# Sums of squares moved between TensorE, POOL and ACT in a four-layer trunk, with a new order of the first loads and of the first projections

## The chip, the cores and the metric

The kernel runs on one core of one Trainium2 chip. The metric is the device time of one execution in microseconds (us), as the median of several runs. The engines are called PE (TensorE matmul), PEld (its weight loads), DVE (VectorE), ACT (ScalarE), POOL (GpSimd) and SP (SyncE, which here only starts transfers).

## The reference

x is 512 positions by 1024 channels in float32. Four layers with the mixers A (Conformer convolution), B (forgetting attention), C (short gated convolution) and A again each add their output to x:

```
hn = rms_norm(x, norm[i]);  x = x + mixer_i(hn)
A: val, gate, z = split(hn @ w_in)            # 3 x 2048 columns
   u = conv31(val * sigmoid(gate)) + b
   u = silu(layer_norm(u, g, b));  out = (u * silu(z)) @ w_out
B: q, k, v, z, f = split(hn @ w_in)           # 16 heads of 128
   q, k = rms_norm(q), rms_norm(k)            # over the 128 of a head
   c = cumsum(log_sigmoid(f + b))
   o = causal softmax(q.k/sqrt(128) + c[t] - c[s]) @ v;  out = (o * silu(z)) @ w_out
C: u, b, c, z = split(hn @ w_in);  out = (b * conv3(c * u) * silu(z)) @ w_out
```

So every layer needs the mean of x squared per position, the A layers also the mean and the mean square of 2048 channels (for layer_norm), and every head of B the mean of q squared and of k squared.

## The kernel before

**Tiles.** Channels lie on the 128 partitions, positions along the free axis. x is 8 tiles of 128x512; the 2048 inner channels are 16 tiles of 128x512. A sum over channels is a sum over partitions and tiles, and is made on PE by a matmul with a matrix of equal constants (`ones_d`, `ones_e`, `ones_h`, and `ones_hr` in fp32r).

**Products in two parts.** Each fp32 operand of a large product is split into a high part in fp32r and the rest, also fp32r. A product is hi·hi + hi·lo + lo·hi: 3 groups of 8 matmuls of 128x512, 24 in all, for each chunk of weights. A chunk of 128x1024 weights is loaded into `w_raw` by SP (a ring of AHEAD = 3), ACT casts it to `w_hi`, and POOL (or DVE) subtracts to give `w_lo` (L413); these two have rings of 4.

**Norms ahead of their sum.** The h of a layer (`hh`, `hl`: x times the norm's gain, split in two) doesn't hold the factor rstd = 1/rms. In B and C the results are multiplied by rstd afterwards. In A only the first four projections (`raw_tiles` = 2: val_0, gate_0, val_1, gate_1) are so treated; from the fifth on, val_2, the operand is `hn` = x·gain·rstd, made by `normalise` once rstd is there. `Stream.add` makes hh, hl and the square of each tile of x, and `norm` sums the squares with `ms` matmuls in fp32 and takes the reciprocal root (ACT Ln and Exp, then three steps on DVE, the last writes `rstdp`).

**Layer A.** The convolution of 31 taps runs as DVE operations (`cv`) and on POOL (`pacc`), a few tiles on PE (`conv_pe`, whose matrices `pw` are loaded by SP). `count_in` adds up each tile's sum and square: POOL sums into s1 and s2, or the tile goes to PE of itself. At the end PE makes `meanp` and `e2p` with fp32 matmuls, and from these come the factor `lnrp`, and per tile `d` → times lnrp → SiLU → times sz → `g_hi`, `g_lo`, which the out projection `o` reads.

**Layer B.** For every head `queries` projects q, takes its square's sum `qs` (L379, by 4 products that have one column of `ones_h` as moving operand) and from it the factor `qr`; `normalise` does the same for k with `ks`. Logits `lg` for four blocks of queries (3 down to 0) give p_3 to p_0 on DVE and ACT; they are scaled by 1/sum on DVE (`rsum`, L350), transposed on PE into `pt`, split, and multiplied with v into `op`.

**Order.** Every operation is handed to a planner (`Plan`). It has a cost for each operation and engine, a priority (place in the program plus `boost`), and the engines that may take it; it simulates the kernel once when it is built, and writes out a fixed order for each engine. An engine works its row in that order, and each instruction waits for what it reads. So any edited cost, boost or engine can move every row behind it.

Of the kernel before, what the change touches and what calls it, by code (L numbers as in the profile page):

```python
# [14 lines left out]
A = mybir.AluOpType  # L15
# [235 lines left out]
def trunk(ctx: ExitStack, tc: tile.TileContext, x, w, vec, pw, out):  # L251
# [41 lines left out]
    def pe_time(n):  # L293
        return max(0.108, 0.0105 + n * 0.4225e-3)
# [100 lines left out]
    def load_chunk():  # L395
        n = state["load"]
        b = plan.buf(lambda: stage.tile([P, 1024], F32, tag="w_raw", name=f"w_raw{n}",
                                        bufs=AHEAD), "w_raw", AHEAD)
        plan.op({"dma": 1.5}, lambda e: nc.sync.dma_start(b(), w[n]), w=[b], boost=-4000 if n >= AHEAD else 0)
        raw_ring[n] = b  # L400
        state["load"] += 1
# [70 lines left out]
    def project(dst, h, fine=False, boost=0):  # L472

        hi, lo = chunk()
        hh, hl = h
        for g, (a, b) in enumerate(((hi, hh), (hi, hl), (lo, hh))):
            for ks in ([k] for k in range(ND)) if fine else [range(ND)]:
                ks = list(ks)
                mms(lambda a=a, b=b, g=g, ks=ks: [
                        (dst(), a()[:, k * P : (k + 1) * P], b[k](),  # L480
                         g == 0 and k == 0, g == 2 and k == ND - 1) for k in ks],
                    [dst], pe_time(T) * len(ks), [a, *(b[k] for k in ks)], boost)

    class Stream:
# [8 lines left out]
        def add(self, d):  # L493
# [7 lines left out]
            act(sq, xs[d], AF.Square, boost=40 if self.layer == 0 else 0)  # L501
            if self.layer == 0 or d in (0, ND - 1):
                self.squares.append(sq)
            else:
                tt(("pool", "dve"), self.squares[0], self.squares[0], sq, A.add)
# [61 lines left out]
    def conformer(layer, st):  # L567
        lo_engines["now"] = ("pool",)
        on_pe = PE_TILES[layer]
        FIRST, EARLY = 2, 7  # L570
        raw_tiles, SPREAD, SHIFTED, DIRECT = 2, 12, 4, 2

        def cw(i, s):
            return v(f"conv_w{layer}", i * KC + KC - 1 - s)

        s1, s2, m0 = slot("s1"), slot("s2"), slot("m0")
        us, d2, sz, last = {}, {}, {}, []
# [75 lines left out]
        def count_in(i):  # L653
# [56 lines left out]
        mp, ep = psum("o", "meanp"), psum("sum", "e2p")  # L710
        for n, (a, b) in enumerate(zip([s1] + [d2[i] for i in range(NE - DIRECT, NE)],
                                       [s2] + last)):
            for dst, src in ((mp, a), (ep, b)):
                mms(lambda n=n, dst=dst, src=src: [
                    (dst(), ones_e(), src(), n == 0, n == DIRECT)], [dst], 0.86, [ones_e, src],
                    boost=-2000)
# [26 lines left out]
    def attention(layer, st):  # L743
# [61 lines left out]
        def queries(h):  # L805
# [6 lines left out]
            act(qh, acc, AF.Copy, scale=g, boost=-200)  # L812
            stt(ql, acc, g, qh, A.mult, A.subtract, boost=-200, b_f32r=True)
            ms = psum("sum", f"qs{h}")
            mms(lambda: [(ms()[:, col(j)], sq()[:, blk(j)], ones_h()[:, :1], True, True)
                         for j in range(NB)], [ms], 0.6, [sq, ones_h])
            m, r, t = fq[h % 2]

            def tiny(op, *bufs, w):
                plan.op({"dve": 0.17}, lambda _: op(), bufs, [w])  # L820
            tiny(lambda: nc.vector.tensor_tensor(m(), ms()[:, :NB], rt2(), A.mult), ms, rt2, w=m)
            plan.op({"act": 0.25}, lambda _: nc.scalar.activation(r(), m(), AF.Ln, bias=eps_t()),
# [219 lines left out]
```

## Time and profile before

| | before |
|---|---|
| median of 3 runs | 1793.65 us (1792.62 to 1793.85) |
| the profiled execution's own time | 1794.22 us |
| its span in the trace | 1792.3 us |
| granted TensorE clock, mean | 0.999 |
| POOL, w_lo, 128x1024 | 274 of 2414 ns |
| ACT, w_hi, 128x1024 | 289 of 1050 ns |
| DVE, cv | 608 of 736 ns |

A line of the profile gives the line of the code, the engine, the operation, written tile <- read tiles, their shape, how often (x), then times. In the lines by time the first number is the start in us from the span's start, the second how long the row lasted (for a row with x3, from the first start to the last end), and in brackets stands idle time ahead of it and what ended that.

The layers lie about so in the span: A from 0 to 402 us, B to 962 (its 16 heads from 410 to 880), C to 1394, A to the end.

### The profile page before, as it was taken

The page shows a single profiled execution, that of the slowest core. Times are in us where ns is not written, and L with a number is a line of the kernel's source. Part 1 is how long each engine was busy: PE and PEld are TensorE (multiplying, and loading weights), DVE is VectorE, ACT ScalarE, POOL GpSimd, SP SyncE. Part 2 cuts the span into 40 slices and gives each one's busy share as a digit, 9 for nine tenths or more (in the row PEclk, how much of TensorE's full clock was granted, in tenths as well). Part 3 has the DMA queues.
Part 4 walks back from the last instruction along what each step waited for, and adds up shares of the span by engine and source line. Part 5 has one row for each costly group of instructions (what it writes and reads, how often), then busy time and mean ns, then how long its engine had stood idle before and what let it go on. Part 6 is the DMA issues. An engine that isn't in the chain of part 4 may idle for free.

```text
span 1792.3 us, 21883 instructions
## 1 busy us (share of the span) xinstructions
PE 1767.3 (99%) x8196; PEld 1462.4 (82%) x8196; DVE 1167.2 (65%) x1690; ACT 866.7 (48%) x1255; POOL 1096.9 (61%) x654
## 2 busy tenths in 40 slices
PE   8999999999999999999999999999999999999999
PEld 6788887888888888888788888888888878878787
DVE  6999997736777777867523333333313699999770
ACT  6656655536555555656433222222223564755550
POOL 5999998865333333544454555455445599989882
PEclk9999999999999999999999999999999999999999
DMA  6243432233222222222222222222223224334222
GB/s 219 83 154 99 141 135 83 94 106 118 83 78 91 85 77 85 75 77 71 71 95 94 94 94 100 101 94 95 96 100 123 88 94 147 106 129 136 94 94 71
DMA packets 63065, 182.40 MB, mean 102 GB/s; under 512 B 7136, under 2 KB 13280, under 8 KB 62960
## 3 DMA queue, kind: packets, MB, share of 16 engines
q1 hardware_dynamic: 62960, 181.02, 29.9%
q8 instruction: 64, 1.05, 0.2%
q14 instruction: 41, 0.34, 0.1%
HBM read 175.71 MB, written 5.28 MB: 101 GB/s over the span
## 4 chain that ended last, share of the span: by engine, by line
PE 81%; DVE 16%; POOL 1%; issue 1%; DMA 1%; ACT 0%; SPq 0%; DVEq 0%; POOLq 0%; ACTq 0%
PE o L379 19%; PE z L379 17%; DVE cv L341 13%; PE k L379 5%; PE v L379 5%; PE u L379 5%; PE c L379 5%; PE b L379 5%; PE q L379 5%; PE gate L379 3%; PE val L379 3%; PE cv L379 2%; PE op L379 2%; PE lg L379 2%; PE pt L874 1%
## 5 line engine op out<-in xcount | busy, mean ns | idle before, releaser
L413 POOL TENSOR_TENSOR w_lo<-w_raw,w_hi 128x1024 fp32r<-128x1024 f32 x274 | 661.1, 2414 | 586.2 <-PE z L379 110.0
L315 ACT CAST w_hi<-w_raw 128x1024 fp32r<-128x1024 f32 x289 | 303.2, 1050 | 550.9 <-issue 137.1
L341 DVE SCALAR_TENSOR_TENSOR cv<-u,vt,cv 128x495 f32<-128x495 f32 (+24 forms) x608 | 447.2, 736 | 19.7
L330 POOL TENSOR_TENSOR pacc<-prod,pacc 128x510 f32<-128x510 f32 (+5 forms) x148 | 174.7, 1181 | 11.1 <-ACT prod L317 4.4
L330 DVE TENSOR_TENSOR x<-o,x 128x512 f32<-128x512 f32 x32 | 21.2, 687 | 200.9 <-PE o L379 200.9
L317 ACT ACTIVATE prod<-u,vt 128x510 f32<-128x510 f32 (+8 forms) x166 | 106.9, 709 | 46.3 <-DVE u L330 46.3
L379 PE MATMUL o<-g_hi,w_hi 128*128 128x512 f32 x512 | 127.9, 391 | 0.7 <-DVE z L330 0.7
L379 PE MATMUL o<-g_lo,w_hi 128*128 128x512 f32 x512 | 127.0, 389 | 0.0
L379 PE MATMUL o<-g_hi,w_lo 128*128 128x512 f32 x512 | 126.7, 389 | 0.0
L379 PEld LDWEIGHTS o<-g_hi,w_hi 128*128 128x128 f32 x512 | 95.8, 188 | 21.7 <-DVE z L330 1.5
L379 PEld LDWEIGHTS o<-g_hi,w_lo 128*128 128x128 f32 x512 | 96.0, 188 | 19.9
L379 PEld LDWEIGHTS o<-g_lo,w_hi 128*128 128x128 f32 x512 | 95.9, 188 | 19.8
L246 ACT ACT_TABLE_LOAD x70 | 89.8, 1283 | 1.9 <-PEq L1030 0.7
L330 DVE TENSOR_TENSOR z<-z,rstd 128x512 f32<-128x512 f32 x32 | 22.1, 691 | 90.2 <-PE z L379 90.1
L379 PE MATMUL z<-hn_hi,w_hi 128*128 128x512 f32 x256 | 65.8, 400 | 2.2 <-ACT sz L317 2.2
L379 PE MATMUL z<-hl,w_hi 128*128 128x512 f32 x256 | 64.6, 394 | 0.0
L379 PE MATMUL z<-hn_hi,w_lo 128*128 128x512 f32 x256 | 64.3, 393 | 0.0
L379 PE MATMUL z<-hh,w_hi 128*128 128x512 f32 x256 | 64.0, 392 | 0.0
L379 PE MATMUL z<-hn_lo,w_hi 128*128 128x512 f32 x256 | 63.7, 391 | 0.0
L379 PE MATMUL z<-hh,w_lo 128*128 128x512 f32 x256 | 63.3, 389 | 0.0
L379 PEld LDWEIGHTS z<-hn_hi,w_hi 128*128 128x128 f32 x256 | 48.1, 191 | 13.9 <-ACT sz L317 3.8
L341 DVE SCALAR_TENSOR_TENSOR hl<-x,vt,hh 128x512 fp32r<-128x512 f32 x32 | 47.6, 1508 | 16.6 <-ACT hh L317 16.6
(245 smaller groups left out, 3708.1 us busy)
## 6 DMA issues: line engine op xcount, KB each, us to landing
w_raw<-w SPq DMA_DIRECT2D x289, 512.0 KB, 3.3
pw<-pw SPq DMA_DIRECT2D x54, 256.0 KB, 4.5
nc<-cd SPq DMA_DIRECT2D x16, 256.0 KB, 3.6
x<-x SPq DMA_DIRECT2D x8, 256.0 KB, 5.2
out<-x SPq DMA_DIRECT2D x8, 256.0 KB, 3.7
ud<-ua SPq DMA_DIRECT2D x6, 256.0 KB, 2.0
phases<-ud SPq DMA_DIRECT2D x24, 64.0 KB, 2.5
od<-oa SPq DMA_DIRECT2D x6, 256.0 KB, 3.9
```

The lines of the kernel that those rows point to most:

```text
L246: switch(table)
L315: nc.scalar.copy(of(dst, d), of(src, s))
L317: nc.scalar.activation(of(dst, d), of(src, s), func, **kw)
L330: eng[e].tensor_tensor(of(dst, d), of(a, s), of(b, sb), op)
L341: nc.vector.scalar_tensor_tensor(of(dst, d), of(a, s), c, bb.bitcast(F32) if b_f32r else bb, op0, op1)
L379: nc.tensor.matmul(o, a, b, start=start, stop=stop)
L413: eng[e].tensor_tensor(lo(), raw(), hi().bitcast(F32), A.subtract)
L874: nc.tensor.transpose(tp()[:, blk(i - j)], p[i]()[:, blk(j)], ident())
```

## The change

1. `queries`: q's square is split into `sq_hi` (ACT) and `sq_lo` (POOL only), and the sum is made by 8 matmuls with two columns of the fp32r constants instead of 4 fp32 products with one column. Its planned cost goes from 0.6 to 0.5 us.
2. `Stream.add`: fewer squares go to PE of themselves. In layer 0 tiles 1 to 3 are added to tile 0's by POOL or DVE (8 `ms` matmuls become 5); in B and C all are added (2 become 1); in the last A layer it stays at 2.
3. `conformer`: of the convolution's 16 tiles only the last one that isn't made on PE (`late`, tile 14) goes to the sums directly, instead of tiles 14 and 15. `meanp` and `e2p` take 2 matmuls each instead of 3.
4. `project` with `fine` (the first projection of each layer): part 7 of h is taken last in all three groups.
5. `load_chunk`: the high priority of a load of weights begins with chunk 6 instead of 3.

```
-        plan.op({"dma": 1.5}, lambda e: nc.sync.dma_start(b(), w[n]), w=[b], boost=-4000 if n >= AHEAD else 0)
+        plan.op({"dma": 1.5}, lambda e: nc.sync.dma_start(b(), w[n]), w=[b], boost=-4000 if n >= 2 * AHEAD else 0)
...
-        for g, (a, b) in enumerate(((hi, hh), (hi, hl), (lo, hh))):
-            for ks in ([k] for k in range(ND)) if fine else [range(ND)]:
-                ks = list(ks)
...
+        groups = list(enumerate(((hi, hh), (hi, hl), (lo, hh))))
+        order = [(g, range(ND)) for g in groups]
+        if fine:
+            order = [(g, [k]) for g in groups for k in range(ND - 1)]
+            order += [(g, [ND - 1]) for g in groups]
+        for (g, (a, b)), ks in order:
...
-            if self.layer == 0 or d in (0, ND - 1):
+            if d == 0 or self.layer == 0 and d >= ND // 2 or LAYERS[self.layer] == "A" and d == ND - 1:
                 self.squares.append(sq)
             else:
                 tt(("pool", "dve"), self.squares[0], self.squares[0], sq, A.add)
...
+        late = max(i for i in range(NE) if i not in on_pe)
...
-            if i < NE - DIRECT:
+            if i != late:
                 tt(("pool",), s1, s1, d2[i], A.add)
                 tt(("pool",), s2, s2, sq, A.add)
...
-        for n, (a, b) in enumerate(zip([s1] + [d2[i] for i in range(NE - DIRECT, NE)],
-                                       [s2] + last)):
+        for n, (a, b) in enumerate(zip([s1, d2[late]], [s2] + last)):
             for dst, src in ((mp, a), (ep, b)):
                 mms(lambda n=n, dst=dst, src=src: [
-                    (dst(), ones_e(), src(), n == 0, n == DIRECT)], [dst], 0.86, [ones_e, src],
+                    (dst(), ones_e(), src(), n == 0, n == 1)], [dst], 0.86, [ones_e, src],
...
+            sp = split(sq, "sq", ("pool",))
             ms = psum("sum", f"qs{h}")
-            mms(lambda: [(ms()[:, col(j)], sq()[:, blk(j)], ones_h()[:, :1], True, True)
-                         for j in range(NB)], [ms], 0.6, [sq, ones_h])
+            mms(lambda: [(ms()[:, 2 * j : 2 * j + 2], b()[:, blk(j)], ones_hr()[:, :2],
+                          b is sp[0], b is sp[1]) for j in range(NB) for b in sp],
+                [ms], 0.5, [*sp, ones_hr])
```

The planner then orders nearly everything anew. Three places matter below.

First, PE at the start of the program. `val_0` is the first projection, `sq` are the squares of the tiles of x, `gate_0` is the second projection. Before, from the eighth row on:

```order
L379 MATMUL ms_139<-sq_146,ones_d_73 128x512
L379 MATMUL val_0_48_126<-hh_5_36_158,w_hi_106 128x512
L379 MATMUL val_0_48_126<-hh_6_39_165,w_hi_106 128x512
L379 MATMUL val_0_48_126<-hh_7_42_171,w_hi_106 128x512
L379 MATMUL val_0_48_126<-hl_0_22_118,w_hi_106 128x512
L379 MATMUL ms_139<-sq_176,ones_d_73 128x512
L379 MATMUL ms_139<-sq_181,ones_d_73 128x512
L379 MATMUL val_0_48_126<-hl_1_25_124,w_hi_106 128x512
L379 MATMUL ms_139<-sq_192,ones_d_73 128x512
L379 MATMUL val_0_48_126<-hl_2_28_135,w_hi_106 128x512
```

Now, the end of val_0 and what follows:

```order
L379 MATMUL val_0_48_126<-hh_7_42_165,w_hi_106 128x512
L379 MATMUL val_0_48_126<-hl_7_43_172,w_hi_106 128x512
L379 MATMUL val_0_48_126<-hh_7_42_165,w_lo_112 128x512
L379 MATMUL ms_209<-sq_122,ones_d_73 128x512
L379 MATMUL ms_209<-sq_201,ones_d_73 128x512
L379 MATMUL ms_209<-sq_207,ones_d_73 128x512
L379 MATMUL ms_209<-sq_211,ones_d_73 128x512
L379 MATMUL ms_209<-sq_216,ones_d_73 128x512
L379 MATMUL gate_0_78_233<-hh_0_21_110,w_hi_178 128x512
```

The eight `ms` matmuls stood between those of val_0; the five now stand in one piece behind it and ahead of gate_0, and the first of them reads sq_122, the sum of four tiles' squares.

Second, POOL at the same place, right behind its constants. Before, its first five rows with work are all low parts of weights (chunks 0 to 4):

```order
L413 TENSOR_TENSOR w_lo_112<-w_raw_96,w_hi_106 128x1024
L413 TENSOR_TENSOR w_lo_161<-w_raw_137,w_hi_153 128x1024
L413 TENSOR_TENSOR w_lo_194<-w_raw_169,w_hi_186 128x1024
L413 TENSOR_TENSOR w_lo_207<-w_raw_183,w_hi_197 128x1024
L413 TENSOR_TENSOR w_lo_254<-w_raw_214,w_hi_234 128x1024
```

Now:

```order
L413 TENSOR_TENSOR w_lo_112<-w_raw_96,w_hi_106 128x1024
L330 TENSOR_TENSOR sq_122<-sq_122,sq_160 128x512
L330 TENSOR_TENSOR sq_122<-sq_122,sq_169 128x512
L413 TENSOR_TENSOR w_lo_191<-w_raw_158,w_hi_178 128x1024
L413 TENSOR_TENSOR w_lo_213<-w_raw_174,w_hi_193 128x1024
```

Two of the three additions stand ahead of the second chunk's low part; the third, `sq_122<-sq_122,sq_186`, stands on DVE behind its eight `hl`.

Third, DVE in a head of B (the third one). `p_3` to `p_0` are the four blocks of the softmax, scaled here by 1/sum; `k_606<-k_605` (now `k_614<-k_613`) is the next head's k projection times rstd. Before:

```order
L350 TENSOR_SCALAR p_2_580_4380<-p_2_580_4380,rsum_435_3867 128x384
L866 RECIPROCAL rsum_434_3877<-rsum_434_3877 128x1
L350 TENSOR_SCALAR p_1_582_4403<-p_1_582_4403,rsum_434_3877 128x256
L866 RECIPROCAL rsum_433_3881<-rsum_433_3881 128x1
L350 TENSOR_SCALAR p_0_584_4422<-p_0_584_4422,rsum_433_3881 128x128
L330 TENSOR_TENSOR k_606_4462<-k_605_4392,rstd_453_3538 128x512
```

Now:

```order
L350 TENSOR_SCALAR p_2_586_4404<-p_2_586_4404,rsum_435_3876 128x384
L330 TENSOR_TENSOR k_614_4484<-k_613_4416,rstd_453_3538 128x512
L871 RECIPROCAL rsum_434_3896<-rsum_434_3896 128x1
L350 TENSOR_SCALAR p_1_588_4427<-p_1_588_4427,rsum_434_3896 128x256
L871 RECIPROCAL rsum_433_3898<-rsum_433_3898 128x1
L350 TENSOR_SCALAR p_0_590_4451<-p_0_590_4451,rsum_433_3898 128x128
```

The k row, which needs the end of a projection on PE, has moved ahead of p_1 and p_0. It is so in every second head; in the others the old order stays. In every head the chunk of v's weights, whose low part DVE made before, now has it made by POOL (11 low parts go from DVE to POOL), and POOL makes the low part of q's square too.

More of the change, by code (lines that the diff above doesn't have):

```diff
@@ L475, in project @@
         hh, hl = h
-        for g, (a, b) in enumerate(((hi, hh), (hi, hl), (lo, hh))):
-            for ks in ([k] for k in range(ND)) if fine else [range(ND)]:
-                ks = list(ks)
[L479 to L482, printed above, removed]
+        groups = list(enumerate(((hi, hh), (hi, hl), (lo, hh))))
[4 more added lines that the diff above has]
+        for (g, (a, b)), ks in order:
+            mms(lambda a=a, b=b, g=g, ks=ks: [
+                    (dst(), a()[:, k * P : (k + 1) * P], b[k](),
+                     g == 0 and k == 0, g == 2 and k == ND - 1) for k in ks],
+                [dst], pe_time(T) * len(ks), [a, *(b[k] for k in ks)], boost)
     class Stream:
@@ L570, in conformer @@
         FIRST, EARLY = 2, 7
-        raw_tiles, SPREAD, SHIFTED, DIRECT = 2, 12, 4, 2
+        raw_tiles, SPREAD, SHIFTED = 2, 12, 4
         def cw(i, s):
             return v(f"conv_w{layer}", i * KC + KC - 1 - s)
+        late = max(i for i in range(NE) if i not in on_pe)
         s1, s2, m0 = slot("s1"), slot("s2"), slot("m0")
@@ L820, in tiny @@
                 plan.op({"dve": 0.17}, lambda _: op(), bufs, [w])
-            tiny(lambda: nc.vector.tensor_tensor(m(), ms()[:, :NB], rt2(), A.mult), ms, rt2, w=m)
+            tiny(lambda: nc.vector.tensor_tensor(m(), ms()[:, : 2 * NB : 2], rt2(), A.mult), ms, rt2, w=m)
             plan.op({"act": 0.25}, lambda _: nc.scalar.activation(r(), m(), AF.Ln, bias=eps_t()),
```

## The prediction

> **What bounds the kernel now.** I read the page's busy times first, then its chain that ended last, both shares of the span of 1792.3 us:
>
> ```profile
> PE 1767.3 (99%) x8196; PEld 1462.4 (82%) x8196; DVE 1167.2 (65%) x1690; ACT 866.7 (48%) x1255; POOL 1096.9 (61%) x654
> ...
> PE 81%; DVE 16%; POOL 1%; issue 1%; DMA 1%; ACT 0%; SPq 0%; DVEq 0%; POOLq 0%; ACTq 0%
> ```
>
> PE is busy in 99% of the span, and the chain lies on it. Only DVE has a share beside it. Where, the view by stretches of the span tells (columns: PE, PEld, DVE, ACT, POOL busy, clock, DMA share, GB/s; the stretches are a part of the first A layer, the heads of B, B's out projection with the first matmuls of C, and C):
>
> ```profile
> 130.00:263.00 133.00, 130.16 (x623) 108.22 (x622) 126.62 (x176) 84.84 (x108) 123.80 (x90) 1.00 0.38 127
> 406.00:880.00 474.00, 470.14 (x2342) 395.01 (x2341) 352.58 (x654) 278.23 (x487) 191.73 (x96) 1.00 0.25 83
> 880.00:964.00 84.00, 84.00 (x377) 69.52 (x377) 20.36 (x22) 27.10 (x34) 44.06 (x20) 1.00 0.28 94
> 964.00:1312.00 348.00, 348.00 (x1534) 287.54 (x1532) 130.12 (x148) 87.24 (x97) 170.41 (x83) 1.00 0.29 97
> ```
>
> In C PE alone is full (348.00 of 348). In A DVE (126.62 of 133) and POOL (123.80) are nearly full too, so their queues decide small waits. In B DVE has room on average, but the softmax is a chain of latencies between PE's products. So PE work that goes away is won, as long as no DVE or POOL result that PE needs comes later by as much.
>
> **The prices.** The critical chain at the start prices the fp32 sum of squares and a projection:
>
> ```profile
> 17.67 2.57 PE ms L379 x6
> 20.25 2.54 PE val L379 x11
> 22.79 5.44 PE gate L379 x24
> ```
>
> A matmul over 512 columns in fp32 is two records (x6 is three): 2.57 / 3 = 0.857 us each. An fp32r matmul is 5.44 / 24 = 0.227 us. The change removes 3 `ms` in layer 0, one each in B and C, and two of `meanp`/`e2p` in each A layer: 9 x 0.857 = **7.7 us** of PE work.
>
> q's squares, before, behind the last logits of a head (PE, then PEld):
>
> ```profile
> 442.65 0.22 PE L379 MATMUL lg<-k_hi,q_hi 128*128 128x128 f32 x1
> 442.71 0.28 PE L379 MATMUL lg<-k_lo,q_hi 128*128 128x128 f32 x1
> 442.82 0.27 PE L379 MATMUL lg<-k_hi,q_lo 128*128 128x128 f32 x1
> 442.94 1.00 PE L379 MATMUL qs<-ones_h,sq 128*128 128x1 f32 x8
> 443.80 1.64 PE L379 MATMUL k<-hl,w_hi 128*128 128x512 f32 x6
> ...
> 442.88 0.97 PEld L379 LDWEIGHTS qs<-ones_h,sq 128*128 128x128 f32 x8
> ```
>
> From 442.94 to 443.80 the 8 passes take 0.86 us, 0.108 each; each must load 128 columns of squares as weights. The new form has 8 fp32r passes with 8 such loads. The nearest rows for those are the logits, fp32r with 128 columns: 0.11 us from start to start (442.71, 442.82, 442.94), also set by the weight load. So 8 x 0.11 = 0.88 against 0.86: **0.0 us**. The best end is 0.06 (442.65 to 442.71 follows a wide matmul, whose time had covered the load): 16 x 8 x 0.05 = 6.4 us won; no reason allows a worse end.
>
> The Trainium skill, page "TensorE: Matmul & The Clock Gate", section on weight-path performance modes, says that fast weight load comes on by itself when 128 weights are loaded and the type isn't FP32. If fp32r counted as another type, the new loads would be quicker than the old ones, and the sum would be by the 0.06 end. The logits' 0.11 in fp32r speaks against it.
>
> **Sums in B and C (-1.7 us).** These lose one `ms` each. The first projection f of B and the POOL work beside it:
>
> ```profile
> 402.79 2.39 POOL L413 TENSOR_TENSOR w_lo<-w_raw,w_hi 128x1024 fp32r<-128x1024 f32 x1 [3.05 <-PE o L379]
> ...
> 406.99 1.98 PE L379 MATMUL f<-hh,w_lo 128*128 128x512 f32 x8
> 408.82 1.02 PE L379 MATMUL ms<-sq,ones_d 128*128 128x512 f32 x2
> ```
>
> The one `ms` now waits for the last addition on POOL. POOL is free at 405.2, an addition takes 1.27 (below), so it ends near 406.5; `ms` is wanted behind f near 408. f's cover of some 1.5 us hides it. -2 x 0.857 = -1.7; if a POOL low part (2.4) came ahead of the addition, 0.9 would be paid in each, +1.8 at worst.
>
> **Statistics in A (-3.4, +0.7).** Two `meanp`/`e2p` go in each A layer: -4 x 0.857 = -3.4. But the four left stand later: 64 matmuls of z lie between them and the out projection, before 80. That is 16 x 0.227 = 3.6 us less for the chain to g. Its slack before:
>
> ```profile
> 298.03 2.54 POOL L330 TENSOR_TENSOR d<-d,mean 128x512 f32<-128x512 f32 x2 [4.45 <-DVE mean L720]
> ...
> 324.70 6.88 DVE L366 TENSOR_TENSOR g_lo<-d,g_hi 128x512 fp32r<-128x512 f32 x4
> ...
> 328.14 1.98 PE L379 MATMUL o<-g_lo,w_hi 128*128 128x512 f32 x8
> ```
>
> The four g_lo (tiles 4 to 7) take 1.72 each, so tile 5's is done at 328.1; PE wants it as the fifth of its eight, at 328.14 + 4 x 0.227 = 329.05. Slack 0.9. The first row prices an addition on POOL, 1.27. In the new order POOL has one low part (2.4) less between the statistics and g_5, so 3.6 - 2.4 - 0.9 = 0.35 us is lost in each A layer: +0.7, between 0 and 2 x 2.7 if that low part doesn't matter.
>
> **The start (+2.5).** Before:
>
> ```profile
> 12.02 3.67 DVE L341 SCALAR_TENSOR_TENSOR hl<-x,vt,hh 128x512 fp32r<-128x512 f32 x3 [0.48 <-ACT hh L317]
> 22.45 0.69 DVE L341 SCALAR_TENSOR_TENSOR nt<-nt,rstd 128x512 f32<-128x512 f32 x1
> 23.18 2.77 DVE L341 SCALAR_TENSOR_TENSOR rstdp<-nt,rstd 128x512 f32<-128x512 f32 x1
> ...
> 22.93 2.47 POOL L413 TENSOR_TENSOR w_lo<-w_raw,w_hi 128x1024 fp32r<-128x1024 f32 x1 [2.69 <-PE val L379]
> ...
> 11.26 1.95 ACT L317 ACTIVATE hh<-x,vt 128x512 fp32r<-128x512 f32 x3
> 16.57 1.67 ACT L317 ACTIVATE sq<-x 128x512 f32<-128x512 f32 x3
> 20.34 0.69 ACT L317 ACTIVATE rstd<-ms,eps_t 128x512 f32<-128x512 f32 x1 [2.10 <-PE ms L379]
> ...
> 22.63 1.75 PE L379 MATMUL gate<-hh,w_hi 128*128 128x512 f32 x7
> ...
> 38.95 1.98 PE L379 MATMUL val<-hn_hi,w_hi 128*128 128x512 f32 x8
> ```
>
> Two things are to be seen. PE gets all of h only at 15.7 (12.02 + 3.67), so the eight `ms` lay partly in val_0's waits. And `rstdp`, which takes two operands from SBUF, lasted 2.77 instead of the 0.69 of `nt`, its like: it ended at 25.95, where POOL's low part had ended at 25.40. A DVE operation of that kind waits for the POOL instruction that runs.
>
> Now val_0 ends at 15.7 + 2 x 0.227, near 16.2. ACT's new row has the first w_hi (to 5.8), eight hh (0.65 each), two sq (0.56), a third, a w_hi (1.0) and the fourth sq: the second sq comes near 11.8, the third near 13.0, the fourth near 14.5. The sum of squares needs two POOL additions (1.27 each, from 11.8 to near 14.4) and one on DVE. This has two SBUF operands and the fourth square, when POOL has just begun the next low part (2.4): it ends at 17.4 to 18.4. Five `ms` (4.3 us) make gate_0 start at 21.7 to 22.7, before 22.63, and the root start near 22.6, before 20.34. So nothing is won for gate_0, and 2.3 us are lost for hn. In the new DVE row the last hn stands behind `raw` of gate_1, whose end is near 38.9, and behind the u made from it: `raw` 0.69, the sigmoid on ACT 0.65, u 0.69 and hn_7 0.69 end near 41.6, its high part near 42.3, and near 42.5 with some tenths between the engines. val_2 wants it at 38.9 + 7 x 0.227 = 40.5: a wait of 2, before none. With the spread of gate_0's start I take +2.5. Ends: -2 (DVE's addition gets in ahead of the low part) and +6 (another low part lies before it and before rstdp).
>
> Part 7 of h taken last and the early x loads are in this sum. In the other layers I put part 7 at nothing: in 880 to 964, which ends in C's first projection, PE is busy in all 84.00 us.
>
> **The heads of B (+6).** Before, DVE and POOL around the end of a k projection, and the last head:
>
> ```profile
> 502.93 0.35 DVE L350 TENSOR_SCALAR p<-p,rsum 128x256 f32<-128x256 f32 x1
> ...
> 503.39 0.29 DVE L350 TENSOR_SCALAR p<-p,rsum 128x128 f32<-128x128 f32 x1
> 505.34 0.69 DVE L330 TENSOR_TENSOR k<-k,rstd 128x512 f32<-128x512 f32 x1 [1.66 <-PE k L379]
> ...
> 876.94 2.31 DVE L350 TENSOR_SCALAR p<-p,rsum 128x256 f32<-128x256 f32 x1
> ```
>
> ```profile
> 505.44 2.41 POOL L413 TENSOR_TENSOR w_lo<-w_raw,w_hi 128x1024 fp32r<-128x1024 f32 x1 [4.71 <-ACT qr L824]
> 507.95 1.30 POOL L366 TENSOR_TENSOR sq_lo<-sq,sq_hi 128x512 fp32r<-128x512 f32 x1
> ...
> 876.71 2.40 POOL L413 TENSOR_TENSOR w_lo<-w_raw,w_hi 128x1024 fp32r<-128x1024 f32 x1 [7.27 <-ACT p L317]
> ```
>
> ```profile
> 505.14 0.93 PE L874 MATMUL pt<-ident,p 128*128 128x128 f32 x7
> ```
>
> p_1 and p_0 were scaled (0.35, 0.29) 1.5 us before k ended and PE transposed them (505.14). Where a low part had begun just ahead, the same operation took 2.31 (876.94 to 879.25; POOL's ended at 879.11). POOL starts one 0.3 us after each k projection's end, since that frees the ring. In 8 of 16 heads the new DVE row puts k's step ahead of p_1 and p_0, so they come behind that low part: its end is k's end + 2.7, then 0.35 + 0.15 + 0.29, so p_0 is there at + 3.5. PE's new row has pt_3, qs, pt_2 and 8 matmuls of v before pt_0: 0.11 + 0.88 + 0.22 + 8 x 0.227 = 3.0. Wait 0.5 each. If POOL's sq_lo (1.30) gets in between p_1 and p_0: 1.8. ACT now makes that sq_hi later, behind pt_2_hi, so I take mostly the first, 0.75: 8 x 0.75 = 6 us; ends 0 and 8 x 1.8 = 14. The weights' low parts that POOL takes over from DVE (11 x 2.4) lie in its idle time, 282 of 474 us in B, and have no price of their own.
>
> **The sum**, against the profiled execution's 1794.22: -1.7 - 3.4 + 0.7 + 2.5 + 6 + 0 = +4.1, 1798.3. That execution is 0.57 above the median 1793.65, so **1797.7** as a median; own range 1793 to 1803.
>
> **Rivals.**
> - *The PE work comes out whole*: no wait at val_2 or pt_0, because POOL's low part starts later than the DVE addition and than p_1. For it: PE is full, and val_0 had 8 `ms` in it. Against: the low part follows k's end by 0.3 us in the rows. It decides by whether p_0 is done within 3.0 us of k's end. 1793.65 - 7.7 = **1785.9**.
> - *Only the heads don't wait*: the start as reckoned. 1797.7 - 6 = **1791.7**.
> - *sq_lo gets in as well* in each of the 8 heads: 1797.7 + 8 = **1806**.
> - *Two-column fp32r passes at 0.06*: 1797.7 - 6.4 = **1791.3**.
>
> **How the numbers follow.** Chances: my forecast 0.42, the whole gain 0.24, no wait in the heads 0.16, sq_lo too 0.13, quick passes 0.05. 0.2% (3.6 us) is about what a measurement of this kernel can tell from no change: faster is below 1790.1, slower above 1797.2. Faster: 0.24, and 0.06 from the two cases near 1791.5: 0.30. Slower: 0.13 and a little over half of the forecast's 0.42: 0.37. The rest is 0.33. The range 1785 to 1804 takes in the whole gain and part of the sq_lo case, and leaves out some 0.15.
>
> **What would show it.** In the new profile: `rstd` near 22.6 (whole gain: before 20.3); a PE wait of about 2 at val_2 for hn; the scaling of p with a maximum near 2.4 in 8 heads, PE waiting there ahead of pt; 8 qs passes in 0.88; `meanp` to the out projection 14.5 instead of 18.2 us, with a small wait for g_lo. I am wrong if the heads keep the 474 us from 406 to 880, or if a stretch that I left alone, A's middle or the loads, moves by more than 3 us.

## The result and the profile after

| | before | after |
|---|---|---|
| median of 5 runs | 1793.65 us (1792.19 to 1795.82) | 1811.44 us (1810.65 to 1817.62) |
| ratio, 95% interval | | 1.0106 [1.0088, 1.0125] |
| span of the profiled execution | 1792.3 us | 1809.3 us |

The change makes the kernel slower by 17.8 us between the medians, about 1% (interval 0.9 to 1.25%). 1797.7 was forecast, and 1804 was the end of the range. The page of after, busy times and the chain that ended last:

```profile
PE 1765.4 (98%) x8178; PEld 1458.1 (81%) x8178; DVE 1169.1 (65%) x1682; ACT 874.2 (48%) x1271; POOL 1151.5 (64%) x687
...
PE 68%; DVE 16%; ACT 1%; issue 1%; DVEq 0%
```

PE has 18 matmul records fewer, yet its busy time fell by 1.9 us only (a busy time also holds matmuls at a lower clock, below). POOL works 54.6 us more; among that are nine of the low parts in the heads, where DVE makes 2 instead of 11, so it is not one in every head. The span is 17.0 longer and PE less busy, so PE waits 18.9 us more. Where, a ledger of single PE instructions tells. Each row is the start of one matmul in both traces:

| PE starts | before | after | later by | in this stretch |
|---|---|---|---|---|
| gate_0 | 22.63 | 25.20 | 2.57 | +2.57 |
| val_2 | 38.95 | 41.96 | 3.01 | +0.44 |
| first z of A | 136.31 | 144.03 | 7.72 | +4.71 |
| first o of A | 315.45 | 319.75 | 4.30 | -3.42 |
| f of B | 402.49 | 410.59 | 8.10 | +3.80 |
| first q of B | 409.27 | 416.50 | 7.23 | -0.87 |
| last chunk of op | 883.47 | 900.28 | 16.81 | +9.58 |
| u of C | 961.60 | 979.31 | 17.71 | +0.90 |
| first o of C | 1311.52 | 1328.35 | 16.83 | -0.88 |
| first o of last A | 1701.39 | 1714.65 | 13.26 | -3.57 |
| end | 1792.33 | 1809.34 | 17.01 | +3.75 |

So three places lose: the start, the heads of B, and the out projections of both A layers. One row says less than it seems to: the -3.57 ahead of the last out projection. In the one trace of the kernel before, PE waits there for a load of `pw`, and the eight matmuls behind it take 3.08 instead of about 2 us, at a granted clock of 0.50 from 1596.90 to 1600.31 us:

```profile
1595.74 2.75 PE L379 MATMUL cv<-phases,pw 128*128 128x126 f32 x16 [3.12 <-DMA pw<-pw]
...
1598.14 3.08 PE L379 MATMUL z<-hn_hi,w_hi 128*128 128x512 f32 x8
```

From the first o of C to the first o of the last A that trace takes 389.87 us. The six later kernels that leave the statistics as they were (e5, e6, e8, e12, e14, e15) take 387.68 to 388.61. So some 1.3 to 2.2 us of each gain on that row belong to this wait in the trace of before, and not to the change.

**The start**, lines by time of after:

```profile
7.20 11.18 DVE L341 SCALAR_TENSOR_TENSOR hl<-x,vt,hh 128x512 fp32r<-128x512 f32 x8 [7.20 <-ACT hh L317]
12.02 3.01 POOL L330 TENSOR_TENSOR sq<-sq,sq 128x512 f32<-128x512 f32 x2 [3.03 <-ACT sq L317]
14.99 10.67 POOL L413 TENSOR_TENSOR w_lo<-w_raw,w_hi 128x1024 fp32r<-128x1024 f32 x4
18.31 2.84 DVE L330 TENSOR_TENSOR sq<-sq,sq 128x512 f32<-128x512 f32 x1
21.20 4.56 PE L379 MATMUL ms<-sq,ones_d 128*128 128x512 f32 x10 [2.03 <-DVE sq L330]
25.80 0.69 ACT L317 ACTIVATE rstd<-ms,eps_t 128x512 f32<-128x512 f32 x1 [3.25 <-PE ms L379]
42.16 0.69 DVE L330 TENSOR_TENSOR raw<-gate,rstd 128x512 f32<-128x512 f32 x1 [0.82 <-PE gate L379]
42.26 2.38 POOL L413 TENSOR_TENSOR w_lo<-w_raw,w_hi 128x1024 fp32r<-128x1024 f32 x1 [3.03 <-ACT cv L317]
43.55 1.63 DVE L330 TENSOR_TENSOR u<-raw,sg 128x512 f32<-128x512 f32 x1
45.11 0.74 DVE L341 SCALAR_TENSOR_TENSOR hn<-x,vt,rstdp 128x512 f32<-128x512 f32 x1
46.52 0.50 PE L379 MATMUL val<-hn_hi,w_hi 128*128 128x512 f32 x1 [2.81 <-ACT hn_hi L315]
46.86 3.50 PE L379 MATMUL val<-hn_lo,w_hi 128*128 128x512 f32 x8
```

The eight hl now end at 18.38 instead of 15.7, because POOL works from 12.02 to 25.66 without a break. Behind them stands the third addition, which lasts 2.84, so `ms` starts at 21.20 after a wait of 2.03. `rstd` comes at 25.80 instead of 20.34. hn_7 stands behind raw and u of gate_1 (45.11; u lasted 1.63 under POOL's low part), and PE waits 2.81 for it. Then eight matmuls take 3.50 instead of 1.98. The view by stretches (clock is the third number from the end) says why:

```profile
44.00:46.00 2.00, 0.00 (x0) 0.00 (x0) 2.00 (x3) 0.78 (x2) 0.64 (x1) 1.00 0.15 33
46.00:48.00 2.00, 1.48 (x4) 1.16 (x5) 1.97 (x4) 2.00 (x4) 0.83 (x1) 0.75 0.59 234
48.00:50.00 2.00, 2.00 (x6) 1.58 (x5) 1.93 (x3) 2.00 (x4) 1.84 (x3) 0.50 0.00 0
```

The granted clock is 0.50 from 46.99 to 50.40 us (0.75 is the mean of a stretch that holds both values), which costs some 1.5 us beside the wait itself. It happens once more from 767.20 to 770.61, behind a wait of 1.8 for k_lo. There it costs nothing: in e5, below, the same wait leaves the clock at 1.00, PE then waits 0.47 and 0.78 for p instead, and the heads take 483.81 us against 483.78 here.

**The heads of B.** One of the eight heads whose k row had moved, by time:

```profile
512.08 0.69 DVE L330 TENSOR_TENSOR k<-k,rstd 128x512 f32<-128x512 f32 x1 [1.10 <-PE k L379]
512.17 2.40 POOL L413 TENSOR_TENSOR w_lo<-w_raw,w_hi 128x1024 fp32r<-128x1024 f32 x1 [2.51 <-ACT p L317]
...
512.87 1.85 DVE L350 TENSOR_SCALAR p<-p,rsum 128x256 f32<-128x256 f32 x1
...
514.52 1.32 POOL L366 TENSOR_TENSOR sq_lo<-sq,sq_hi 128x512 fp32r<-128x512 f32 x1
514.64 0.15 DVE L871 RECIPROCAL rsum<-rsum 128x1 f32<-128x1 f32 x1
514.83 1.10 DVE L350 TENSOR_SCALAR p<-p,rsum 128x128 f32<-128x128 f32 x1
...
515.99 0.99 PE L879 MATMUL pt<-ident,p 128*128 128x128 f32 x7 [0.90 <-DVE p L350]
```

p_1 lasts until POOL's low part is done (514.57 and 514.72), and p_0 until POOL's sq_lo is done (515.84 and 515.93). From v's last matmul to pt_0 there are 1.29 us where 0.23 would do: 1.06 lost, the same in seven of the eight, 7.4 in all. In the first of them p_1 and p_0 are not held up (0.36 and 0.29), and PE doesn't wait. The view of waits by what is waited for, 406 to 900 us (total, times, longest; the 11 waits are these seven and four others):

```profile
PE pt L879 <- DVE p L350: 8.5, 11, 0.9
PE lg L379 <- DVE k_lo L366: 1.8, 1, 1.8
```

**The out projection of A**, by time:

```profile
299.88 1.30 POOL L330 TENSOR_TENSOR s<-s,d 128x512 f32<-128x512 f32 x1
301.13 1.28 POOL L330 TENSOR_TENSOR s<-s,sq 128x512 f32<-128x512 f32 x1
301.79 1.02 PE L379 MATMUL meanp<-s,ones_e 128*128 128x512 f32 x2
...
319.63 1.30 POOL L330 TENSOR_TENSOR d<-d,sz 128x512 f32<-128x512 f32 x1 [2.60 <-ACT d L317]
320.89 2.41 POOL L413 TENSOR_TENSOR w_lo<-w_raw,w_hi 128x1024 fp32r<-128x1024 f32 x1
323.26 11.10 POOL L330 TENSOR_TENSOR d<-d,sz 128x512 f32<-128x512 f32 x7
...
327.54 1.20 PE L379 MATMUL o<-g_hi,w_hi 128*128 128x512 f32 x4 [1.27 <-ACT g_hi L315]
327.73 2.10 DVE L413 TENSOR_TENSOR w_lo<-w_raw,w_hi 128x1024 fp32r<-128x1024 f32 x1
329.75 5.16 DVE L366 TENSOR_TENSOR g_lo<-d,g_hi 128x512 fp32r<-128x512 f32 x3
331.56 1.20 PE L379 MATMUL o<-g_lo,w_hi 128*128 128x512 f32 x4 [1.91 <-DVE g_lo L366]
```

Tile 15's two additions stand late on POOL, and the statistics behind them. Then one low part stands on POOL between the first and the second `d`·sz, and one on DVE ahead of three g_lo. PE waits for g_hi and for g_lo. The last A layer repeats it (waits of 1.25 and 1.92).

### The profile page after: what moved, and what is told of

The parts are those of the page before. It is cut to its first block, busy times and chain, and to the rows that moved or that the text cites. A ratio compares the mean times of both kernels' runs of the same rounds, so it can differ in the third digit from the quotient of the medians.

```text
span 1809.3 us, 21921 instructions
## 1 busy us (share of the span) xinstructions
PE 1765.4 (98%) x8178; PEld 1458.1 (81%) x8178; DVE 1169.1 (65%) x1682; ACT 874.2 (48%) x1271; POOL 1151.5 (64%) x687
## 4 chain that ended last, share of the span: by engine, by line
PE 68%; DVE 16%; ACT 1%; issue 1%; DVEq 0%
PE o L379 18%; PE z L379 13%; DVE cv L341 9%; PE c L379 5%; PE u L379 5%; PE b L379 5%; PE k L379 5%; PE q L379 4%; PE v L379 4%; DVE p L350 2%; PE op L379 2%; PE lg L379 1%; PE cv L379 1%; PE gate L379 1%; DVE d L330 1%; PE pt L879 1%
## 5 line engine op out<-in xcount | busy, mean ns | idle before, releaser
L413 POOL TENSOR_TENSOR w_lo<-w_raw,w_hi 128x1024 fp32r<-128x1024 f32 x285 | 689.4, 2420 | 525.3 <-PE o L379 78.7
L379 PE MATMUL val<-hn_hi,w_hi 128*128 128x512 f32 x224 | 55.8, 390 | 2.8 <-ACT hn_hi L315 2.8
```

The lines of the kernel that those rows point to most:

```text
L379: nc.tensor.matmul(o, a, b, start=start, stop=stop)
L413: eng[e].tensor_tensor(lo(), raw(), hi().bitcast(F32), A.subtract)
```

## The experiments

All times are medians, each with the kernel before on the same chip. "Parts" are those of the list in the section on the change.

| run | kernel | us | ratio to before |
|---|---|---|---|
| e5 | part 1 alone | 1803.05 | 1.0051 [1.0034, 1.0068] |
| e1 | change, k behind p_0 | 1806.11 | 1.0071 [1.0056, 1.0086] |
| e14 | e12, part 1, k behind p_0 | 1795.45 | 1.0002 [0.9992, 1.0011] |
| e15 | e14, sq_lo on DVE | 1799.72 | 1.0024 [1.0015, 1.0034] |
| e6 | part 2 alone | 1800.49 | 1.0037 [1.0024, 1.0050] |
| e2 | change, layer 0's squares as before | 1804.03 | 1.0058 [1.0043, 1.0073] |
| e9 | change without layer 0's additions | 1807.99 | 1.0077 [1.0063, 1.0091] |
| e13 | change, hn_7 ahead of gate_1's raw | 1801.87 | 1.0041 [1.0029, 1.0054] |
| e4 | parts 1, 2, 3 | 1806.28 | 1.0069 [1.0052, 1.0086] |
| e7 | part 3 alone | 1793.74 | 0.9997 [0.9988, 1.0006] |
| e3 | change, g's steps at higher priority | 1808.07 | 1.0081 [1.0066, 1.0096] |
| e10 | change without tile 15's additions | 1805.00 | 1.0066 [1.0051, 1.0082] |
| e8 | sums of B and C alone | 1792.34 | 0.9989 [0.9980, 0.9999] |
| e11 | e12, part 3, e3's priority | 1794.69 | 1.0002 [0.9993, 1.0011] |
| e12 | parts 4, 5, sums of B and C | 1791.48 | 0.9984 [0.9975, 0.9993] |

### The heads: e5, e1, e14, e15

**e5**: before with part 1 alone, the core of it:

```
+            sp = split(sq, "sq", ("pool",))
...
-            mms(lambda: [(ms()[:, col(j)], sq()[:, blk(j)], ones_h()[:, :1], True, True)
+            mms(lambda: [(ms()[:, 2 * j : 2 * j + 2], b()[:, blk(j)], ones_hr()[:, :2],
```

> The kernel before with part 1 alone: q's squares in two fp32r parts, sq_lo on POOL. Theory (part 1 is what turns the heads' order, and with it costs about 1.06 us in 8 heads and some 1 to 3 more in B): +9.6, 1803.7 beside 1794.1, between 1801 and 1806. Rival (the heads lose only together with the other parts): 1793 to 1797.

1803.05; the span is 9.2 longer. q's first matmul stands where it stood (-0.33), the last chunk of op is 9.29 later, C's u 10.19. That is 9.6 in the heads, as in after: their whole loss comes with part 1, whatever the rest does.

**e1**: the change, with k's step on DVE kept behind the last scaled block of the head before:

```
-            tt(("dve",), f, acc, st.rstd, A.mult, boost=-200)
+            tt(("dve",), f, acc, st.rstd, A.mult, boost=-200,
+               after=[scaled[h - 1]] if name == "k" and h else ())
...
+            scaled[h] = p[0]
```

> The changed kernel with one dependence more: a head's k times rstd waits for the scaled p_0 of the head before, so DVE's row has k behind p_1 and p_0 in all heads, as before the change. Everything else of the change stays, q's squares in two parts too. Theory (p_1 and p_0 fall behind POOL's low part in 8 heads, about 1.06 us each at pt_0): 1811.4 - 8.5 = 1803, between 1800 and 1805. Rival (q's squares cost time by themselves, on PE or as POOL's additional low part, and the order of DVE's rows is a side effect): 1809 to 1812.

1806.11, 5.3 less than after, measured in different batches. The same head in e1:

```profile
511.91 0.35 DVE L350 TENSOR_SCALAR p<-p,rsum 128x256 f32<-128x256 f32 x1
...
512.00 2.50 POOL L413 TENSOR_TENSOR w_lo<-w_raw,w_hi 128x1024 fp32r<-128x1024 f32 x1 [2.51 <-DVE rsum L874]
...
512.37 2.22 DVE L350 TENSOR_SCALAR p<-p,rsum 128x128 f32<-128x128 f32 x1
```

p_1 takes 0.35 again, since it starts 0.09 ahead of the low part. p_0 still falls into it. In the seven heads PE now waits 0.25 at the fifth of the seven transposes instead of 1.06 ahead of the first, and 0.1 to 0.2 more at the two ks matmuls behind them. The heads cost +4.8 instead of +9.6. So half of their loss is the place of k's row; 8.5 had been expected of it, a miss, and the other half I had not expected.

**e14** asks whether that half belongs to part 1, free of the rest: e12 (below), with part 1 and e1's edit.

> The kernel of e12 (1791.5) with q's squares in two parts added, and k behind the scaled p_0 of the head before. Theory (the k row costs 4.8 of the 9.6 that B loses; the other 4.8 are small waits that come with part 1 by itself): 1791.5 + 4.8 = 1796.3, between 1795 and 1798. Rival (they came from the other parts): 1791 to 1793.

From the first q to the last op it loses 4.8 against e12, as expected. Its PE row shows: seven waits of 0.25 among the transposes (1.8) with 0.1 to 0.2 more at ks behind each (1.0), two of 0.66 ahead of pt_0, where POOL's low part holds p_0 for 2.45, one of 0.55 at ks, waits of 2.0, 1.1 and 0.4 in the heads from 752 us on, and seven matmuls at half clock behind the first of those (1.4): some 9.5. e12 has some 4.6 of such waits there. The difference, 4.9, is about what was to be explained.

**e15**: e14 with the low part of q's square on DVE instead of POOL:

```
-            sp = split(sq, "sq", ("pool",))
+            sp = split(sq, "sq", ("dve",))
```

> As e14, with sq_lo of q's squares on DVE instead of POOL. Theory (the remaining waits come from POOL, whose additional low part blocks DVE's operations on p, pt and k): at least half of 4.8 goes, 1792 to 1794.5. Rival (they come from the new places of qs and pt in PE's row, whoever makes sq_lo): within 1 of e14.

1799.72, 4.3 more, outside of both ranges; the heads lose 8.5 instead of 4.8. So taking sq_lo off POOL in this way wins nothing, and on DVE it costs more. How much of the remaining half POOL's sq_lo makes is not shown by it, since DVE's row is another one too.

### The start: e2, e9, e13, e4, e6

**e2**: the change, with all eight squares of layer 0 on PE:

```
-            if d == 0 or self.layer == 0 and d >= ND // 2 or LAYERS[self.layer] == "A" and d == ND - 1:
+            if d == 0 or self.layer == 0 or LAYERS[self.layer] == "A" and d == ND - 1:
```

> The changed kernel with the squares of layer 0 again all summed on PE (8 ms matmuls); the sums of B and C, the early loads of x and part 7 taken last stay. Theory (the start loses by the sum of squares that waits for POOL and DVE, which are blocked by each other and by the low parts): gate_0 starts near 23 and val_2 doesn't wait; 1811.4 - 7.7 = 1803.7, between 1802 and 1806. Rival (the start loses by the loads in the new order or by part 7 last, PE's first matmul being 0.65 later already): 1809 or more.

1804.03. gate_0 starts at 22.73, val_2 at 39.05 without a wait, z is 1.38 later than before instead of 7.72. So 6.3 of the 7.7 that the start loses come from adding layer 0's squares. The first out projection also loses 2.1 less (below).

**e9**: the change, the three additions of layer 0 not issued (`if self.layer:` ahead of the `tt` of part 2).

> The changed kernel with the three additions of squares in layer 0 left out (the squares of tiles 1 to 3 don't enter the first norm's sum); four ms matmuls of tiles 4 to 7 and one of tile 0 remain. Theory (the additions, and DVE's and POOL's waits for each other, hold up the sum and with it gate_0 and hn): val_0 ends near 16.5, the root starts near 20, val_2 waits less than 0.5; z's first matmul within 2 us of the kernel before; 1811.4 - 7 = 1804, between 1802 and 1806. Rival (it is the place of the five ms matmuls and of part 7 behind val_0): 1809 or more.

1807.99. val_0 ends at 16.6 and gate_0 starts at 16.47, as I had reckoned val_0's end. The eight hl are done at 14.42 instead of 18.38:

```profile
7.43 6.99 DVE L341 SCALAR_TENSOR_TENSOR hl<-x,vt,hh 128x512 fp32r<-128x512 f32 x8 [7.43 <-ACT hh L317]
```

So the additions hold up the hl behind POOL, not only the sum. But PE still waits for hn_7, and longer:

```profile
42.03 0.68 PE L379 MATMUL val<-hn_hi,w_hi 128*128 128x512 f32 x1 [3.79 <-ACT hn_hi L315]
```

rstd is there at 21.92, early; hn_7 waits for its place on DVE, behind gate_1's u. Half a miss: that place is a cause of its own.

**e13**: the change, with gate_1's `raw` kept behind hn_7:

```
-                tt(("dve",), f, acc, st.rstd, A.mult, boost=-2500)
+                tt(("dve",), f, acc, st.rstd, A.mult, boost=-2500,
+                   after=[normal[0][ND - 1]] if name == "gate" and i else ())
```

> The changed kernel with one dependence more: gate_1's product with rstd on DVE waits for the high part of hn_7, so that DVE's row has hn_7 ahead of it and of the u made from it. The additions of squares, the five ms behind val_0 and all else stay. Theory (val_2 waits because hn_7 stands behind gate_1's end in DVE's row, and the pause of 3 us then halves the granted clock for about 3 us): gate_0 stays near 25, val_2 doesn't wait and the clock stays at 1.00: 1811.4 - 4.6 = 1806.8, between 1805 and 1808.5. Rival (the late sum alone holds up hn_7): the wait stays, 1810 or more.

1801.87 (1801.31 to 1806.62), 3 us below the expected range. val_2 has no wait and the clock stays at 1.00 there. The new order also makes each out projection lose 1.7 instead of 3.8 in its trace, which I had not counted on. Its profiled execution, which took 1806.62, shows another thing, at the first sums (lines by time, then stretches):

```profile
21.16 7.53 PE L379 MATMUL ms<-sq,ones_d 128*128 128x512 f32 x10 [2.03 <-DVE sq L330]
```

```profile
19.00:21.00 2.00, 0.14 (x1) 0.00 (x0) 2.00 (x1) 0.00 (x0) 2.00 (x2) 0.84 0.90 334
21.00:23.00 2.00, 1.84 (x2) 0.83 (x3) 0.11 (x1) 1.04 (x1) 2.00 (x1) 0.50 0.73 270
23.00:25.00 2.00, 2.00 (x4) 0.94 (x3) 0.00 (x0) 0.00 (x0) 2.00 (x2) 0.50 0.66 225
```

The same pause of 2.03 as in after, but here the clock was 0.50 from 20.36 to 27.18 and the five sums took 7.53 instead of 4.56.

**e4**: the change without parts 4 and 5, so the first projection in three groups of eight and the loads as before.

```
-        plan.op({"dma": 1.5}, lambda e: nc.sync.dma_start(b(), w[n]), w=[b], boost=-4000 if n >= 2 * AHEAD else 0)
+        plan.op({"dma": 1.5}, lambda e: nc.sync.dma_start(b(), w[n]), w=[b], boost=-4000 if n >= AHEAD else 0)
```

> The changed kernel without its parts 4 and 5: the loads and the first projections in the order of before. Theory (sums in layer 0 are what the start loses by): gate_0 still starts 2 or more later than before and val_2 still waits 2 or more; 1809 to 1813. Rival (the loads or part 7 last): the start is as before, 1803 to 1805.

1806.28, a miss: I had expected the wait at val_2 to stay. gate_0 is 4.3 later than before (clock 0.72 and 0.50 in 19 to 23 us, the sums 5.81), but nothing waits at val_2. Up to the first z it still loses 7.76, as after does (7.72), so parts 4 and 5 are not what the start loses by; the time below after comes mostly from the out projections, which lose 1.7 each instead of 3.8.

**e6**: before with part 2 alone (its one line of the diff).

> The kernel before with part 2 alone: fewer ms matmuls, sums on POOL and DVE. Theory (the start loses about 4.3 by the sums alone, as seen at val_2 with parts 4 and 5 undone, and B and C win 0.86 each): +2.6, 1796.7, between 1795 and 1799. Rival (the sums cost only together with the new order of loads): 1791 to 1793.

1800.49, a miss by 3.8. Its profile is of its fastest execution, 1797.03. There gate_0 is 5.95 later than before, val_2 5.98; B and C gain 0.6 each. PE runs at half pace from its first matmul to 25.3 us (0.43 a matmul, five sums in 6.18), where before it had full pace by 13.8. So the sums at the start lose without parts 4 and 5 too, by other waits each time.

### The statistics: e7, e3, e10

**e7**: before with part 3 alone.

```
-            if i < NE - DIRECT:
+            if i != late:
```

> The kernel before with part 3 alone: two matmuls each for the statistics, two more additions on POOL in each A layer. Theory (POOL, 93% busy in A, pays 2 x 1.27 us, and the chain to g loses what PE wins): within 1 of the kernel before, 1793 to 1796. Rival, my recorded term (-3.4 + 0.7): 1791.4, between 1790 and 1792.5.

1793.74, no difference, as stated: -2.2 to the first o, +1.7 in the first out projection; -3.3 and +1.7 in the last, where some of the -3.3 is the wait in the trace of before. So it gives back 3.4, as much as the four matmuls save. Its profile also has 1.6 us more in B's heads near 758, by the clock alone (below).

**e3**: the change, with the steps of g_2 to g_5 at a higher priority:

```
-            boost = -2500 + 10 * k if first else 0
+            boost = -2500 + 10 * k if first else -400 if k < 6 else 0
```

> The changed kernel with the chain of g for tiles 2 to 5 of an A layer given priority over the low parts of weights (boost -400). The statistics stay at two matmuls each, 64 matmuls ahead of the out projection. Theory (the waits of 1.4 and 2.1 us in each A layer come from one low part on POOL between two of the products d times sz, and one on DVE ahead of g_3's low part): both waits go, 1811.4 - 7.0 = 1804.4, between 1803 and 1807. Rival (the chain from the statistics to g is simply 3.6 us too long for 64 matmuls, whatever lies between): at least 1808.

1808.07. The waits at g_3 and g_4 go, others come later (0.66, 0.26, 0.83), and each out projection loses 2.3 instead of 3.8. Its time is the rival's, its trace lies between theory and rival. Most of it is moved, not won.

**e10**: the change, tile 15's two additions on POOL not issued.

```
-            if i != late:
+            if i == NE - 1:
+                pass
+            elif i != late:
```

> The changed kernel without the two POOL additions of tile 15 to s1 and s2 in each A layer (tile 15 doesn't enter the layer norm's statistics); two matmuls each as in the change. Theory (these additions, 2.5 us on a POOL that is 93% busy, are what makes the statistics late, so that only 64 matmuls of z are left to cover the chain to g): the statistics stand 80 or more matmuls ahead of the out projection, its waits of 3.5 go in both A layers; 1811.4 - 7.0 = 1804.4, between 1802.5 and 1806. Rival (the POOL row of low parts is the cause, whatever the additions do): waits of 2 or more remain, 1808 or more.

1805.00. The last statistics now have 88 matmuls of z behind them (80 in the last layer) instead of 64, and both out projections lose nothing (o 3.15 later, f 3.15 later; 8.75 and 8.74 in the last). POOL still has a low part behind the first `d`·sz:

```profile
313.02 1.29 POOL L330 TENSOR_TENSOR d<-d,sz 128x512 f32<-128x512 f32 x1 [2.60 <-ACT d L317]
314.28 2.41 POOL L413 TENSOR_TENSOR w_lo<-w_raw,w_hi 128x1024 fp32r<-128x1024 f32 x1
316.64 11.15 POOL L330 TENSOR_TENSOR d<-d,sz 128x512 f32<-128x512 f32 x7
```

So the low part hurts only since the statistics are late, and they are late by these additions. Where they are late, the order on POOL goes with the size: with two `d`·sz ahead of that low part (e4, e7, e13, the first of e2) an out projection loses 1.7, though only 56 matmuls of z stand behind the statistics; with one (after, e9, the first of e1, the last of e2) it loses 3.8.

The same trace shows something else, at the start, which this edit leaves alone: PE's row is that of after up to 280 us, and still gate_0 starts at 22.83 instead of 25.20.

```profile
6.93 9.06 DVE L341 SCALAR_TENSOR_TENSOR hl<-x,vt,hh 128x512 fp32r<-128x512 f32 x8 [6.93 <-ACT hh L317]
11.84 3.59 POOL L330 TENSOR_TENSOR sq<-sq,sq 128x512 f32<-128x512 f32 x2 [3.13 <-ACT sq L317]
```

Here the sixth hl began at 11.83, just ahead of POOL's first addition, and only the last two were held up (0.74, then 1.78 and 1.78). In after it began at 12.11, behind POOL's 12.02, and three were (1.78, 1.76, 2.88). So some 2.4 us of the start hang on 0.1 us, in one and the same order.

### What is left that wins: e8, e11, e12

**e8**: before with the additions of B and C only (e2's line).

> The kernel before with the single ms matmul in B and C alone (layer 0 and the last A layer as before). Theory: PE is full there and the addition on POOL is hidden: -1.7, 1792.4, between 1791.5 and 1793.2. Rival (the addition on POOL delays the root and the planner's new order costs elsewhere): 1794 or more.

1792.34; 0.6 won at B and 0.6 at C, as stated, and again 1.6 lost near 758 in its profile. Another 2.2 are won in the last A layer, which the edit leaves alone: there before's trace has its wait for `pw`, 3.12 against 1.74 here, and the half clock.

**e11**: parts 3, 4 and 5, B's and C's sums, and e3's priority; q and layer 0 as before.

> Parts 3, 4 and 5, the single ms in B and C, layer 0's squares on PE as before, q's squares as before, and the chain of g given priority: what the runs so far found not to lose. From the stages: A -1.6 by the first q, B and C -0.9 each (one of them in the -1.6), the last A layer between -1 and 0: 1794.4 - 3 = 1791.4, between 1789.5 and 1793. Rival (every new order brings its own waits): 1794 or more.

1794.69, a miss: the first out projection loses 4.6, by a wait of 2.17 for g_lo ahead of 323.50 and eight matmuls at half clock behind it, the last 2.4.

**e12**: as e11 without part 3 and the priority.

> Parts 4 and 5 and the single ms in B and C, layer 0's squares on PE, the statistics and q's squares as before. Expected from the sums in B and C alone (-2.0 in the trace of that run) and no price of parts 4 and 5 at the start (gate_0 +0.1 where layer 0's squares were on PE): 1792.4, between 1791 and 1793.5. Rival (parts 4 and 5 win or lose by themselves): below 1790.5 or above 1794.

1791.48, below before by 2.9 us, with an interval that leaves 1 out. It is the lowest median of all, though its interval and that of e8 overlap. In its profiled execution, the shortest with 1789.47, gate_0 starts 1.37 earlier than before, q 2.66, C's out projection 3.55, and the end is 4.81 earlier; B and C give 0.88 each of that. Parts 4 and 5 do no harm where the squares of layer 0 stay on PE; that they win is not shown.

## Why the prediction was off, step by step

- **Sums in B and C, -1.7**: right. -0.87 and -0.88 in the ledger.
- **q's squares on PE, 0.0**: right. In after the first of the 8 passes starts at 511.90 and pt behind them at 512.80, 0.90 against 0.86. The rival of passes at 0.06 falls: fp32r loads here keep fp32's pace, as the logits' rows had it. With it falls, for these loads, the fast weight load that the Trainium skill gives to types other than FP32 (page "TensorE: Matmul & The Clock Gate", weight-path performance modes).
- **The start, +2.5, was +7.7.** The mechanisms were named rightly: a DVE addition held up by POOL, a late root, hn_7 behind gate_1's u. Two terms were too small. The step "val_0 ends at 15.7 + 2 x 0.227" counted POOL's hold on the addition and on rstdp, but not on the hl ahead of them: they ended at 18.38, and all behind came 2.5 to 3.5 later (gate_0 at 25.20 for 21.7 to 22.7; in e10's trace, with the same rows there, it was 22.83). e9 shows val_0's end where I had put it once the additions are gone. And the wait of 2 was 2.81 and took the clock with it, some 1.5 more. The upper end of this term, +6, was meant for one more low part; that was too low as well.
- **The heads, +6, were +9.6**, and 0.9 more up to C. The first half is the term itself: p_1 and p_0 behind the low part. I had priced it between 0.5 (low part alone) and 1.8 (sq_lo too). sq_lo did get in, in seven heads, yet the wait was 1.06: p_0 was done 3.9 after k's end (512.04 to 515.93), where that case had 3.5 + 1.3 = 4.8. p_1 ended 0.15 and p_0 0.09 behind POOL's instruction, so p_1's own 0.35 and p_0's 0.29 don't come on top. 7 x 1.06 = 7.4. Undoing the place of k's row gave back 4.8 of 9.6: those waits shrank by 7 x 0.81 = 5.7, and 0.1 to 0.2 in each head came back at ks. The other half had no term at all: part 1's new order, with the rest of these waits, others at the transposes and at ks, and a pause near 765 (found in e14's PE row).
- **Statistics in A.** -3.4 of PE work: right. The ledger has another -3.6 on the way to the out projections: 1.7 in the first A layer, which e12 and e14, with the statistics as before, have too, and 1.9 in the last, where the trace of before had its wait for `pw`. **The +0.7 was +7.5**, the worst step. It said "POOL has one low part (2.4) less between the statistics and g_5" and took 3.6 - 2.4 - 0.9. The 16 matmuls less were right (64, before 80). But the rows behind were not those of before: a low part came between two `d`·sz, another on DVE ahead of g_lo, and there are waits of 1.4 and 2.1 in place of one of 0.35. I had put the upper end at 2.7 per layer; it was 3.8. e10 shows the cause, e7 that part 3 alone gives back 3.4, as much PE work as it saves.
- **Parts 4 and 5 at nothing**: right where layer 0's squares stay on PE (e12); where they don't, the start loses the same without them (e4).

The sum by these sizes: 7.7 - 3.4 + 3.8 - 0.9 + 9.6 + 0.9 - 0.9 - 3.6 + 3.8 = +17.0, the difference of the spans.

Of the rivals, that sq_lo gets in too (1806) came nearest, by its mechanism, at 7.4 us in seven heads instead of the 14 that it priced. That its total lay nearest is luck: the start and the statistics made up the rest. The whole gain of 7.7 us of PE work did happen, and was more than given back.

## What to carry to other kernels

Where PE is 99% busy, a few matmuls less are worth what the engine that takes over the work can give: here POOL took 54.6 us of new work, and its instructions also held up DVE's. Work moved to such an engine has to be followed to every DVE row that may run beside it, the unedited ones too, and a PE wait of about 2 us has to be priced with the slower clock that may follow it. What won were the additions whose sum has a projection on PE as cover (B's and C's, 0.6 to 0.9 each). And a ledger of two traces holds the chance waits of both: the trace of before has to be read for them too.

## What the runs showed of the hardware

The granted clock fell to 0.50 around short pauses of PE: behind one of 2.81 us and one of 1.8 us in the changed kernel (46.99 to 50.40 and 767.20 to 770.61 us), and with one of 2.03 us in e13 (20.36 to 27.18). With the same 2.03 us in the changed kernel it stayed at 1.00. One wait shows it best, that for p ahead of a head's third logits, 1.92 to 1.95 us in before, e6, e7, e8, e11 and e12 alike. In before the clock stays at 1.00 and the eight matmuls of k behind it take 2.00; in e8 this stands there:

```profile
757.59 0.38 PE L379 MATMUL lg<-k_hi,q_hi 128*128 128x256 f32 x1 [1.92 <-DVE p L341]
...
758.19 3.40 PE L379 MATMUL k<-hh,w_hi 128*128 128x512 f32 x8
```

The wait costs 1.6 us more in the heads in two of the six (e7 and e8). The traces tell which. All changes of the clock in a trace lie whole multiples of 3.413 us apart (in the changed kernel at 12.86, 46.99, 50.40, 767.20 and 770.61), in each of the 17 traces, so each trace can be cut into a grid of stretches of 3.41 us. Two stretches of this grid in before, then two in e8:

```profile
753.81:757.22 3.41, 2.75 (x13) 2.01 (x11) 3.41 (x4) 2.85 (x5) 3.41 (x3) 1.00 0.46 156
757.22:760.63 3.41, 2.15 (x11) 1.88 (x12) 3.34 (x9) 2.43 (x5) 2.56 (x1) 1.00 0.00 0
```

```profile
754.37:757.78 3.41, 1.49 (x8) 0.96 (x6) 3.38 (x5) 2.89 (x4) 3.41 (x3) 1.00 0.40 148
757.78:761.19 3.41, 3.41 (x11) 2.73 (x11) 3.31 (x10) 2.93 (x8) 1.10 (x1) 0.50 0.36 119
```

In before an edge of the grid splits the wait; in e8 it lies in one stretch, PE is busy for only 1.49 of 3.41 us in that, and the next stretch is at half clock. Over all traces, their last few us aside, the clock fell 20 times, each time at the end of a stretch in which PE had been busy for 1.89 us or less, 18 of them with 1.59 or less. It stayed at 1.00 in three stretches with 1.58 or 1.59, and in all the others PE was busy for 1.70 or more. In the same way the first full clock of every trace came at the end of a stretch in which PE was busy for at least 3.19 us, and not behind those before it, with 2.90 or less. That is e6's slow start: its short waits left 2.53 to 2.77 in four stretches running, and the first full one ended at 25.32 us, against 13.12 in before.

The Trainium skill, page "TensorE: Matmul & The Clock Gate", Part 1 on the HAM clock gate, has the half clock come after an idle window of about 3.4 us, and that window free-running. The length of the window and its free phase agree with these runs (3.413 us); but here PE need not be idle for all of it, pauses of 1.5 to 1.9 us in it could be enough.

A stretch of 3.41 us at half clock lowers the mean clock of an execution by 3.41 x 0.5 / 1792 = 0.001. Of the 21 executions of before beside e13, the five with a mean of 1.000 took 1792.80 to 1792.95 us, the six with 0.997 took 1797.03 to 1798.56. The changed kernel's longest execution (1817.62) has 0.995, its others (1810.65 to 1813.18) 0.998. The spread of e13 (1801.31 to 1806.62) doesn't follow it, with 1804.09 at 1.000 and 1801.69 at 0.998; its cause stays open.
